# Low parts of 21 weight tiles from an adding transfer instead of a VectorE subtraction

## The chip, the core and the metric

The kernel runs on one core of a Trainium2 chip. The metric is the device time of one execution in microseconds, as the median of several runs. Engines are named as the profile names them: PE is TensorE, DVE is VectorE, ACT is ScalarE, POOL is GpSimd and SP is SyncE.

## What is computed

A decoder of two layers on 512 positions of width 1024, in f32. A layer has a first gated feed-forward part, a token mixer (layer 0: latent attention beside gated linear attention, layer 1: stick-breaking attention), a second feed-forward part, and a gate that adds the layer's embedding. Cut to the parts that the change touches:

```python
def rms_norm(x, w):
    return x * lax.rsqrt(jnp.mean(x * x, axis=-1, keepdims=True) + EPS) * w

def swiglu_ffn(h, w_gu, w_down):
    a, b = jnp.split(h @ w_gu, 2, axis=-1)
    return (jax.nn.silu(a) * b) @ w_down

# each layer i
x += 0.5 * swiglu_ffn(rms_norm(x, ffn1_norm), ffn1_w_gu, ffn1_w_down)
x += W_out [ MLA(h) || GLA(h) ]           # layer 0, h = rms_norm(x)
x += W_out StickBreaking(h)               # layer 1
x += 0.5 * swiglu_ffn(rms_norm(x, ffn2_norm), ffn2_w_gu, ffn2_w_down)
x += sigmoid(rms_norm(x) W_g) * (p[i] W_p)
```

## The kernel before

The activations are kept transposed: eight tiles x0 to x7 of 128 features by 512 positions. A product in f32 is made of three products in the matmul format fp32r. Each operand is split into a high part (rounded to fp32r) and a low part (the operand minus its high part), and `mm3` issues high by high (L393), high weight by low activation (L394) and low weight by high activation (L395) into one PSUM accumulator.

The weights come in tiles of 128 by up to 1024. One such tile is one block of 128 output columns with all its 1024 input rows, so it serves 24 matmuls of 512 positions. The list `plan` names the tiles in the order in which the program uses them. `weight(key)` hands out the next one and keeps two rings going ahead of it: `w_load` issues a load from SP into a raw tile wr (8 buffers, or 5 while plain tiles are loaded), and `w_split` makes the two parts, up to four tiles ahead (`WS`), in tiles wh and wl. For a plain tile `w_split` calls `w_cut`: ACT casts the high part (L260) and DVE subtracts (L261). Three tiles of the mixers' outputs and the last layer's gate are held in slabs instead (kh and kl, L313 and L314), and the groups "sg" of the feed-forward parts are combined on DVE before they are split (L289).

Three kinds of plain tile matter here:

- **"gu"**: five column blocks of gate and up projection of layer 0's first feed-forward part, ten tiles. `start` splits the first two in pieces of 256 columns (`FIRST` is 2). `gates` uses the other eight, A and B in turn. When `norm.row()` has made R, the inverse norm in all partitions (ACT's copy at L507), DVE multiplies A and B by it (L790, L793) before the nonlinearity.
- **"pg"**: the eight tiles of the gate of the embedding in layer 0 (`ple`), used as accumulators G. DVE's instructions in this stage are kept in program order, and the profile puts all of them at L123. Behind the gate the next norm's steps run: nu, nw and their parts (nuh by ACT at L562), and the sum of squares sqa, which TensorE reduces at L587.
- **"oo"**: the output projection of the odd mixer (layer 1). Tiles 0 to 2 are held in slabs, tiles 3 to 7 are plain. They are taken while the attention heads still run: a head makes scores z, soft values u (ACT L1508 to L1510, DVE L1512), their parts soh and sol, sums la of u over column blocks by POOL (L1521, L1522), whose parts are lah (ACT L399) and lal (DVE L401), and the next head's sqk with parts sqkh and sqkl. TensorE reads lal at L1537 and sqkl at L395.

The order on each engine is set by the scheduler that lays out the program, from what each instruction depends on and which ring buffers come free; an engine works through its list in that order and waits on semaphores. POOL has little to do in the kernel: the la sums, some casts of constants and a few loads that it issues (L376).

Of the kernel before, what the change touches and what calls it, by code (L numbers as in the profile page):

```python
# [13 lines left out]
AF = mybir.ActivationFunctionType  # L14
ALU = mybir.AluOpType
# [93 lines left out]
def tile_kernel(ctx: ExitStack, tc: tile.TileContext, a: dict, out: bass.AP):  # L109
    nc = tc.nc  # L110
    act, dve, pe, pool = nc.scalar, nc.vector, nc.tensor, nc.gpsimd
# [27 lines left out]
    def sl(p, dt=F32):  # L139
        return slab.tile([P, S], dt, tag="s", name=nm(p))  # L140
# [4 lines left out]
    def bank(p="ps"):  # L145
        return ps.tile([P, S], F32, tag="b", name=nm(p))

    def f32(t):
        return t.bitcast(F32)


    plan = []
# [70 lines left out]
    raw, ready = {}, {}  # L223
    at = [0, 0, 0]
    FIRST = 2
# [3 lines left out]
    loads, needs, done = [], [], []  # L229
    base, grouped = {}, set()  # L230
    for key in plan:
# [7 lines left out]
        if g not in base:  # L239
# [3 lines left out]
            n = 2 * groups_of(w_, l_)[g_][1]  # L243
            src = a[f"sg{w_}{l_}{g_}"]
# [14 lines left out]
    def w_cut(t, n, hi, lo, cs, pin=lambda ins: ins):  # L259
        pin(act.copy(hi[:, cs], t[:, cs]))  # L260
        pin(dve.tensor_tensor(lo[:, cs], t[:, cs], f32(hi)[:, cs], op=ALU.subtract))  # L261

    def w_tiles():
        hi = wp.tile([P, WCOLS], F32R, tag="wh", name=nm("wh"), bufs=WS)
        lo = wp.tile([P, WCOLS], F32R, tag="wl", name=nm("wl"), bufs=WS)
        return hi, lo

    def kept(i):

        k = plan[i]  # L270
        return k[0] == "pgl" or (k[0] in ("eo", "oo") and k[1] < OPEN)

    def wc(w, o):
        return w[o // S][:, o % S : o % S + P] if isinstance(w, list) else w[:, o : o + P]

    def w_pin(key):


        if key[3] == 0 and key[4] == "T1":
            return tc.keep_in_program_order  # L280
        return lambda ins: ins

    def w_term(key):

        _, _, _, _, term, u = key
        b0 = base[key[:4]]
        (b11, n), (b21, _), (b12, _), (b22, _) = [raw.get(b0 + 2 * b + u, (None, 0)) for b in range(4)]
        pin = w_pin(key)
        sub = lambda o, x, y: pin(dve.tensor_tensor(o[:, :n], x[:, :n], y[:, :n], op=ALU.subtract))  # L289
        if term == "T1":  # L290
            sub(b11, b12, b11)
        elif term == "T2":
            sub(b11, b22, b11)
        elif term == "T3":
            sub(b12, b22, b12)
        elif term == "T4":
            sub(b21, b21, b11)
        return {"B11": b11, "B21": b21, "T1": b11, "T2": b11, "B22": b22, "T3": b12, "T4": b21}[term], n

    def w_split():  # L300
        i = at[1]
        if plan[i][0] == "sg":
            t, n = w_term(plan[i])
            ready[i] = w_tiles()
            w_cut(t, n, *ready[i], slice(0, n), w_pin(plan[i]))
            at[1] += 1
            return
        t, n = raw.pop(needs[i] - 1)
        if kept(i):
            parts = [[sl("kh", F32R) for _ in range(2)], [sl("kl", F32R) for _ in range(2)]]  # L310
            for c in range(2):
                src = t[:, c * S : c * S + S]
                act.copy(parts[0][c], src)  # L313
                dve.tensor_tensor(parts[1][c], src, f32(parts[0][c]), op=ALU.subtract)  # L314
            ready[i] = parts
        else:
            ready[i] = w_tiles()
            w_cut(t, n, *ready[i], slice(0, n))
        at[1] += 1

    def weight(*key):
        assert plan[at[2]] == key, (plan[at[2]], key)
        while True:
            of = done[at[1] - 1] if at[1] else 0
            if at[0] < len(loads) and at[0] - of < (WR if at[0] in grouped else WR_PLAIN):
                w_load()
            elif at[1] < len(plan) and at[1] < at[2] + WS and needs[at[1]] <= at[0]:
                w_split()
            else:
                break  # L330
        k = plan[min(at[1], len(plan) - 1)][0]
        for _ in range(BURST.get(k, 0)):
            if at[1] < at[2] + AHEAD and at[1] < len(plan) and needs[at[1]] <= at[0] and kept(at[1]):
                w_split()
        got = ready.pop(at[2])
        at[2] += 1
        return got
# [302 lines left out]
    def start(norm):  # L640

        table("silu_and_others")
        warm = bank("warm")
        for _ in range(WARM):
            pe.matmul(warm, ones_r, ones_r[:, 0:1].to_broadcast([P, S]), start=True, stop=True)
# [1011 lines left out]
def groups_of(w, l):  # L1657

    if (w, l) == (1, 0):
        return [(KC * P, 384), (KC * P + 384, 384)]  # L1660
    return [(0, 512), (512, 512), (1024, 384)]
# [10 lines left out]

EV = (0, 2, 4, 6, 1, 3, 5, 7)
OPEN = 3
WARM = 8
AHEAD = 5
BURST = {"eo": 2, "oo": 1, "pgl": 1}
# [56 lines left out]
def build(arrays):  # L1734
    import concourse.bacc as bacc

    nc = bacc.Bacc("TRN2", target_bir_lowering=False, num_devices=1, dynamic_dma_scratch_size=4096)
    a = {
        n: nc.dram_tensor(f"in_{n}", list(v.shape), mybir.dt.from_np(v.dtype), kind="ExternalInput").ap()
        for n, v in arrays.items()  # L1740
    }
    out = nc.dram_tensor("out", [S, D], F32, kind="ExternalOutput").ap()
    with tile.TileContext(nc) as tc:
        tile_kernel(tc, a, out)
    return nc
# [9 lines left out]
```

## Time and profile before

| | |
|---|---|
| median of three runs | 1315.92 us |
| the three runs | 1312.94, 1319.41, 1315.92 us |
| the profiled execution | 1318.16 us |
| its span, first to last instruction | 1316.4 us |
| busy PE, DVE, ACT, POOL | 1280.7, 910.8, 665.1, 116.9 us |
| DVE's subtractions at L261, all weights | 292 rows, 312.7 us |
| ACT's casts at L260 | 299 rows, 275.4 us |

All rows are of the one profiled execution. A row of a timeline gives the start, the duration, the engine, the line, the operation with what it writes and reads, and in brackets how long the engine had been idle and what released it. Where several like instructions follow one another the row gives their number and their whole time. A matmul's duration overlaps the next one's, so the distance of starts is the rate. Lines of kept instructions of DVE are shown as L123.

### The profile page before, as it was taken

The page shows a single profiled execution, that of the slowest core. Times are in us where ns is not written, and L with a number is a line of the kernel's source. Part 1 is how long each engine was busy: PE and PEld are TensorE (multiplying, and loading weights), DVE is VectorE, ACT ScalarE, POOL GpSimd, SP SyncE. Part 2 cuts the span into 40 slices and gives each one's busy share as a digit, 9 for nine tenths or more (in the row PEclk, how much of TensorE's full clock was granted, in tenths as well). Part 3 has the DMA queues.
Part 4 walks back from the last instruction along what each step waited for, and adds up shares of the span by engine and source line. Part 5 has one row for each costly group of instructions (what it writes and reads, how often), then busy time and mean ns, then how long its engine had stood idle before and what let it go on. Part 6 is the DMA issues. An engine that isn't in the chain of part 4 may idle for free.

```text
span 1316.4 us, 16266 instructions
## 1 busy us (share of the span) xinstructions
PE 1280.7 (97%) x6212; PEld 1092.2 (83%) x6212; DVE 910.8 (69%) x1316; ACT 665.1 (51%) x1064; POOL 116.9 (9%) x132
## 2 busy tenths in 40 slices
PE   9969999998999999999989999999999999999997
PEld 7869888886888888988868898888888887898886
DVE  6688763579775998654799875445767598885544
ACT  6455352432654565542655553334778556554442
POOL 0001000425350000000000000000111000000000
PEclk9979999999899999999989999999999999999999
DMA  7023343111300032533203343322113003224401
GB/s 290 34 88 117 109 147 106 45 64 41 121 17 17 0 128 97 160 128 111 81 1 128 97 129 111 128 97 96 65 59 102 16 16 128 93 85 142 145 1 64
DMA packets 39454, 118.66 MB, mean 90 GB/s; under 512 B 4615, under 2 KB 5768, under 8 KB 39376
## 3 DMA queue, kind: packets, MB, share of 16 engines
q1 hardware_dynamic: 38016, 114.64, 26.2%
q0 software_dynamic: 640, 1.89, 0.5%
q8 instruction: 49, 0.80, 0.2%
q10 hardware_dynamic: 720, 1.09, 0.2%
q14 instruction: 29, 0.24, 0.1%
HBM read 115.50 MB, written 2.10 MB: 89 GB/s over the span
## 4 chain that ended last, share of the span: by engine, by line
PE 87%; DVE 9%; ACT 2%; issue 1%; SPq 0%; DMA 0%; POOL 0%; POOLq 0%; DVEq 0%; ACTq 0%
PE dn L395 6%; PE dn L394 6%; PE dn L393 6%; PE al L704 5%; PE al L705 5%; PE al L706 5%; PE ga L705 3%; PE ga L704 3%; PE ga L706 3%; PE sqk L393 2%; PE sqk L395 2%; PE sqk L394 2%; PE val L1016 2%; PE val L1018 2%; PE val L1017 2%; DVE wl L261 1%
## 5 line engine op out<-in xcount | busy, mean ns | idle before, releaser
L260 ACT CAST wh<-wr 128x1024 fp32r<-128x1024 f32 (+3 forms) x299 | 275.4, 925 | 362.2 <-PE dn L394 81.5
L261 DVE TENSOR_TENSOR wl<-wr,wh 128x1024 fp32r<-128x1024 f32 (+3 forms) x292 | 312.7, 1075 | 168.1 <-ACT wh L260 167.4
L395 PE MATMUL dn<-gh,wl 128*128 128x512 f32 x352 | 137.4, 390 | 0.3 <-DVE wl L261 0.2
L393 PE MATMUL dn<-gh,wh 128*128 128x512 f32 x352 | 137.0, 392 | 0.7 <-ACT wh L260 0.7
L394 PE MATMUL dn<-gl,wh 128*128 128x512 f32 x352 | 137.2, 390 | 0.0
L289 DVE TENSOR_TENSOR wr<-wr,wr 128x1024 f32<-128x1024 f32 (+1 forms) x88 | 94.9, 1097 | 0.2
L395 PEld LDWEIGHTS dn<-gh,wl 128*128 128x128 f32 x352 | 66.1, 188 | 14.9 <-DVE wl L261 1.2
L393 PEld LDWEIGHTS dn<-gh,wh 128*128 128x128 f32 x352 | 66.0, 188 | 14.5 <-ACT wh L260 1.1
L394 PEld LDWEIGHTS dn<-gl,wh 128*128 128x128 f32 x352 | 66.1, 188 | 13.8 <-DVE gl L401 0.6
L602 POOL TENSOR_TENSOR rc<-v,half 128x4 f32<-128x4 f32 x8 | 11.8, 1480 | 683.5 <-DVE v L600 683.5
L704 PE MATMUL al<-wh,nvh 128*128 128x512 f32 (+1 forms) x176 | 64.6, 367 | 4.7 <-ACT nvh L534 4.7
L705 PE MATMUL al<-wl,nvh 128*128 128x512 f32 (+1 forms) x176 | 64.5, 366 | 0.0
L706 PE MATMUL al<-wh,nvl 128*128 128x512 f32 (+1 forms) x176 | 64.3, 367 | 0.0
L637 DVE SCALAR_TENSOR_TENSOR x<-dn,x 128x512 f32<-128x512 f32 x32 | 22.1, 691 | 40.9 <-PE dn L395 40.9
L393 PE MATMUL sqk<-xnh,wh 128*128 128x512 f32 x128 | 50.2, 393 | 0.0
L395 PE MATMUL sqk<-xnh,wl 128*128 128x512 f32 x128 | 50.0, 390 | 0.0
L394 PE MATMUL sqk<-xnl,wh 128*128 128x512 f32 x128 | 49.9, 390 | 0.0
L704 PE MATMUL ga<-wh,nuh 128*128 128x512 f32 (+1 forms) x88 | 34.6, 406 | 6.3 <-ACT wh L260 6.3
L704 PEld LDWEIGHTS al<-wh,nvh 128*128 128x128 f32 x176 | 33.2, 189 | 8.9 <-ACT nvh L534 5.1
L481 ACT ACTIVATE sq<-x 128x512 f32<-128x512 f32 x64 | 39.2, 622 | 0.0
L1016 PE MATMUL val<-wh,xnh 128*128 128x512 f32 x96 | 37.5, 391 | 0.0
L1018 PE MATMUL val<-wh,xnl 128*128 128x512 f32 x96 | 37.4, 389 | 0.0
(462 smaller groups left out, 3293.6 us busy)
## 6 DMA issues: line engine op xcount, KB each, us to landing
wr<-in_sg SPq DMA_DIRECT2D x48, 512.0 KB, 4.0
wr<-in_sg SPq DMA_DIRECT2D x40, 384.0 KB, 3.3
wr<-in_dn SPq DMA_DIRECT2D x32, 384.0 KB, 3.1
wr<-in_dn SPq DMA_DIRECT2D x32, 320.0 KB, 3.5
wr<-in_od_qk SPq DMA_DIRECT2D x16, 512.0 KB, 3.2
wr<-in_ev_in SPq DMA_DIRECT2D x12, 512.0 KB, 3.5
wr<-in_gu SPq DMA_DIRECT2D x8, 512.0 KB, 7.2
wr<-in_ev_out SPq DMA_DIRECT2D x8, 512.0 KB, 3.2
```

The costliest lines, as they stand in the source:

```text
L260: pin(act.copy(hi[:, cs], t[:, cs]))
L261: pin(dve.tensor_tensor(lo[:, cs], t[:, cs], f32(hi)[:, cs], op=ALU.subtract))
L289: sub = lambda o, x, y: pin(dve.tensor_tensor(o[:, :n], x[:, :n], y[:, :n], op=ALU.subtract))
L393: pe.matmul(acc, wh, xh, start=start, stop=False, **k)
L394: pe.matmul(acc, wh, xl, start=False, stop=False, **k)
L395: pe.matmul(acc, wl, xh, start=False, stop=stop, **k)
L481: ins = act.activation(sq, x[m], AF.Square)
L704: pe.matmul(o, h[:, cs], wh[:, ws], start=begin, stop=False, skip_group_check=True)
L705: pe.matmul(o, h[:, cs], wl[:, ws], start=False, stop=False, skip_group_check=True)
L706: pe.matmul(o, lw[:, cs], wh[:, ws], start=False, stop=end, skip_group_check=True)
L1016: pe.matmul(accs[b], xn[k][0][:, bs], wh[:, ws], start=k == 0, stop=False)
L1018: pe.matmul(accs[b], xn[k][1][:, bs], wh[:, ws], start=False, stop=k == KD - 1)
```

## The change

The new function `w_cut_dma` makes the two parts of a tile without DVE. ACT casts the high part as before, ACT writes its negative into the low part's tile, and POOL issues a transfer that reads the weight once more from memory and adds it onto that tile. `w_split` calls it for every plain tile of "pg", "oo" and "gu" except the two of `start`: eight of "gu", eight of "pg" and five of "oo". What is kept in slabs, and all other weights, are split as before.

```diff
+    def w_cut_dma(t, src, n, hi, lo):
+        act.copy(hi[:, :n], t[:, :n])
+        act.activation(lo[:, :n], f32(hi)[:, :n], AF.Copy, scale=-1.0)
+        pool.dma_start(lo[:, :n], src, accum_op=ALU.add)
...
             ready[i] = parts
+        elif plan[i][0] in BY_DMA and needs[i] > FIRST:
+            ready[i] = w_tiles()
+            w_cut_dma(t, loads[needs[i] - 1][0], n, *ready[i])
         else:
             ready[i] = w_tiles()
             w_cut(t, n, *ready[i], slice(0, n))
...
+BY_DMA = ("pg", "oo", "gu")
```

Over the program DVE has 21 rows fewer, ACT 21 more and POOL 21 more, and SP's list is the same. In the new program L260 stands for the casts of `w_cut`, L279 and L280 for the cast and the negation of `w_cut_dma`, L281 for its transfer; later lines are ten higher. The scheduler also moves rows on the other engines. Three places follow; the numbers behind a name count its buffers and differ between the two programs.

The first is PE in `gates`, at the first tile that `start` did not split: A_61 with wh_31 and wl_32, then B_65 and A_69 with the next tiles. Before:

```order
L393 MATMUL A_61_296<-xnh_10_127,wh_31_236 128x512
L394 MATMUL A_61_296<-xnl_11_129,wh_31_236 128x512
L395 MATMUL A_61_296<-xnh_10_127,wl_32_237 128x512
L393 MATMUL A_61_296<-xnh_12_141,wh_31_236 128x512
L394 MATMUL A_61_296<-xnl_13_143,wh_31_236 128x512
L395 MATMUL A_61_296<-xnh_12_141,wl_32_237 128x512
L393 MATMUL A_61_296<-xnh_14_155,wh_31_236 128x512
L394 MATMUL A_61_296<-xnl_15_157,wh_31_236 128x512
```

Now:

```order
L403 MATMUL A_61_300<-xnh_10_127,wh_31_236 128x512
L404 MATMUL A_61_300<-xnl_11_129,wh_31_236 128x512
L403 MATMUL B_65_332<-xnh_10_127,wh_34_243 128x512
L404 MATMUL B_65_332<-xnl_11_129,wh_34_243 128x512
L403 MATMUL A_69_364<-xnh_10_127,wh_37_250 128x512
L404 MATMUL A_69_364<-xnl_11_129,wh_37_250 128x512
L405 MATMUL A_61_300<-xnh_10_127,wl_32_237 128x512
L403 MATMUL A_61_300<-xnh_12_141,wh_31_236 128x512
L404 MATMUL A_61_300<-xnl_13_143,wh_31_236 128x512
L405 MATMUL A_61_300<-xnh_12_141,wl_32_237 128x512
```

The first products of the next two accumulators are moved ahead of the first one that reads wl_32.

The second is POOL in the odd mixer, the sixth and the seventh of the eight heads (la_1884 and la_1887 are the sixth's, la_1931 and la_1934 the seventh's). Before:

```order
L1521 COPY la_1884_8634<-u_1876_8608 128x128
L1522 TENSOR_TENSOR la_1884_8634<-u_1876_8608,u_1875_8607 128x128
L1521 COPY la_1887_8641<-u_1875_8607 128x128
L1522 TENSOR_TENSOR la_1887_8641<-u_1875_8607,la_1884_8634 128x256
L1521 COPY la_1931_8823<-u_1923_8797 128x128
L1522 TENSOR_TENSOR la_1931_8823<-u_1923_8797,u_1922_8796 128x128
L1521 COPY la_1934_8830<-u_1922_8796 128x128
L1522 TENSOR_TENSOR la_1934_8830<-u_1922_8796,la_1931_8823 128x256
```

Now:

```order
L281 DMA wl_1945_8885<-in_od_out 128x1024
L1531 COPY la_1884_8650<-u_1876_8624 128x128
L1532 TENSOR_TENSOR la_1884_8650<-u_1876_8624,u_1875_8623 128x128
L281 DMA wl_1949_8908<-in_od_out 128x1024
L1531 COPY la_1887_8657<-u_1875_8623 128x128
L1532 TENSOR_TENSOR la_1887_8657<-u_1875_8623,la_1884_8650 128x256
L281 DMA wl_1965_8980<-in_od_out 128x1024
L281 DMA wl_1987_9072<-in_od_out 128x1024
L1531 COPY la_1931_8839<-u_1923_8813 128x128
L1532 TENSOR_TENSOR la_1931_8839<-u_1923_8813,u_1922_8812 128x128
L1531 COPY la_1934_8846<-u_1922_8812 128x128
L1532 TENSOR_TENSOR la_1934_8846<-u_1922_8812,la_1931_8839 128x256
```

Four transfers now stand between the la operations: of tile 3 ahead of the first pair, of tile 4 ahead of the second, of tiles 5 and 6 ahead of the four of the seventh head.

The third is ACT at the end of the embedding's gate, where wh_1282 and wh_1299 are weights of the next feed-forward part and nuh belongs to its norm. Before:

```order
L260 CAST wh_1282_5799<-wr_1187_5389 128x1024
L546 ACTIVATE noh_1263_5735<-x3_75,gains_70 128x512
L813 ACTIVATE gt_1271_5773<-gt_1271_5773 128x512
L260 CAST wh_1299_5867<-wr_1195_5436 128x1024
L562 CAST nuh_1272_5780<-nu_1265_5738 128x512
L563 CAST nwh_1252_5679<-nw_1251_5678 128x256
L481 ACTIVATE sq_1273_5783<-x3_75 128x512
L546 ACTIVATE noh_1274_5787<-x5_77,gains_70 128x512
```

Now:

```order
L556 ACTIVATE noh_1263_5751<-x3_75,gains_70 128x512
L260 CAST wh_1282_5815<-wr_1187_5401 128x1024
L823 ACTIVATE gt_1271_5789<-gt_1271_5789 128x512
L572 CAST nuh_1272_5796<-nu_1265_5754 128x512
L573 CAST nwh_1252_5695<-nw_1251_5694 128x256
L491 ACTIVATE sq_1273_5799<-x3_75 128x512
L260 CAST wh_1299_5883<-wr_1195_5448 128x1024
L556 ACTIVATE noh_1274_5803<-x5_77,gains_70 128x512
```

The cast of wh_1299 is moved behind nuh_1272 and the two instructions after it; noh_1263 comes ahead of wh_1282.

## Rows read from the trace of the kernel before

**Rows 1.** The page: busy time by engine, and the chain that ended last.
```profile
PE 1280.7 (97%) x6212; PEld 1092.2 (83%) x6212; DVE 910.8 (69%) x1316; ACT 665.1 (51%) x1064; POOL 116.9 (9%) x132
...
PE 87%; DVE 9%; ACT 2%; issue 1%; SPq 0%; DMA 0%; POOL 0%; POOLq 0%; DVEq 0%; ACTq 0%
```

**Rows 2.** Windows; columns: us, PE, PEld, DVE, ACT, POOL busy, clock, DMA share, GB/s.
```profile
0.00:43.00 43.00, 41.19 (x169) 32.33 (x170) 24.81 (x40) 22.64 (x34) 2.99 (x8) 1.00 0.66 238
...
992.00:1003.70 11.70, 11.70 (x59) 9.92 (x58) 8.69 (x14) 11.43 (x23) 2.29 (x4) 1.00 0.41 134
1013.30:1020.90 7.60, 7.60 (x36) 6.28 (x35) 5.11 (x9) 7.60 (x16) 2.30 (x4) 1.00 0.23 73
```

**Rows 3.** Timeline of DVE; columns: start us, us, line, operation, [idle before <-releaser].
```profile
43.26 0.68 DVE L790 TENSOR_TENSOR a<-A,R 128x512 f32<-128x512 f32 x1
...
654.57 1.23 DVE L123 TENSOR_TENSOR wl<-wr,wh 128x1024 fp32r<-128x1024 f32 x1 [0.57 <-ACT wh L260]
...
667.33 0.69 DVE L123 TENSOR_TENSOR nul<-nu,nuh 128x512 fp32r<-128x512 f32 x1 [0.93 <-ACT nuh L562]
...
1004.27 0.89 DVE L401 TENSOR_TENSOR lal<-la,lah 128x256 fp32r<-128x256 f32 x2
...
1008.43 0.69 DVE L401 TENSOR_TENSOR sqkl<-sqk,sqkh 128x512 fp32r<-128x512 f32 x1 [0.69 <-ACT sqkh L399]
...
1062.76 0.69 DVE L635 TENSOR_TENSOR x<-x,oo 128x512 f32<-128x512 f32 x1 [0.65 <-PE oo L395]
```

**Rows 4.** Timeline of ACT: casts of the third plain gate tile and the first pg.
```profile
15.20 1.05 ACT L260 CAST wh<-wr 128x1024 fp32r<-128x1024 f32 x1 [0.42 <-DMA wr<-in_gu]
...
602.42 1.06 ACT L260 CAST wh<-wr 128x1024 fp32r<-128x1024 f32 x1 [2.35 <-PE dn L394]
```

**Rows 5.** Timeline of POOL: a transfer issued from it.
```profile
81.46 0.61 POOL L376 DMA_DIRECT2D craw<-in_consts  x1 [44.51 <-DVE nwl L569]
```

**Rows 6.** Transfers: KB each, median us to landing.
```profile
wr<-in_gu SPq DMA_DIRECT2D x8, 512.0 KB, 7.2
wr<-in_pg SPq DMA_DIRECT2D x8, 512.0 KB, 3.2
...
craw<-in_consts POOLq DMA_DIRECT2D x3, 256.0 KB, 3.1
```

**Rows 7.** Timeline of PE: third tile's first products, and pg's first low part.
```profile
18.35 0.39 PE L393 MATMUL A<-xnh,wh 128*128 128x512 f32 x1
18.58 0.39 PE L394 MATMUL A<-xnl,wh 128*128 128x512 f32 x1
...
613.06 0.39 PE L395 MATMUL G<-xnh,wl 128*128 128x512 f32 x1
```

**Rows 8.** Timeline of PE behind the embedding's gate.
```profile
685.42 1.75 PE L587 MATMUL pss<-ones,sqa 128*128 128x2 f32 x8 [1.98 <-DVE sqa L123]
```

**Rows 9.** Windows behind three stops of PE.
```profile
299.00:306.00 7.00, 6.71 (x37) 5.74 (x38) 6.78 (x17) 1.08 (x2) 0.00 (x0) 1.00 0.01 2
685.00:692.50 7.50, 7.08 (x21) 5.56 (x22) 6.85 (x9) 5.53 (x8) 1.92 (x1) 0.54 0.00 1
1090.00:1096.00 6.00, 5.46 (x20) 4.13 (x21) 6.00 (x8) 4.72 (x6) 1.93 (x1) 0.72 0.00 0
```

**Rows 10.** Timeline of ACT behind the last plain gate tile.
```profile
41.99 0.58 ACT L507 COPY R<-wide 128x512 f32<-128x512 f32 x1
```

**Rows 11.** Timeline of POOL in the odd mixer, sixth head.
```profile
1000.58 0.76 POOL L1521 COPY la<-u 128x128 f32<-128x128 f32 x1
1001.30 0.91 POOL L1522 TENSOR_TENSOR la<-u,la 128x256 f32<-128x256 f32 x1
```

**Rows 12.** Timeline of ACT in the odd mixer, sixth head.
```profile
1002.91 0.82 ACT L399 CAST lah<-la 128x256 fp32r<-128x256 f32 x2
```

**Rows 13.** Timeline of PE in the odd mixer, sixth head.
```profile
1008.06 0.34 PE L1537 MATMUL z<-lal,cr 128*128 128x384 f32 x1
...
1011.35 0.34 PE L395 MATMUL z<-sqkh,sqkl 128*128 128x384 f32 x1
```

## The prediction

> **What bounds the kernel now.** The page first: TensorE is busy for 97% of the span, VectorE for 69%, and the chain that ended last is 87% TensorE and 9% VectorE [rows 1]. So freed VectorE time is worth something only where TensorE waits for VectorE. The windows by stage come next, since the 21 tiles lie in three places: in the first 43 us TensorE is busy for 41.19 us while VectorE needs 24.81, and the DMA engines are busy for 0.66; in two stretches of the odd mixer TensorE never stops, and ScalarE is busy for 11.43 of 11.7 us and for all of 7.6 us [rows 2]. There the change adds work to a full engine and takes it from one that has room. The timelines then give lengths and waits one by one.
>
> **What is removed.** 21 subtractions of 1.23 us (each as the one at 654.57 [rows 3]) leave VectorE, some 26 us. The eight of the plain gates gain nothing: TensorE is the full engine there. The eight of the embedding's gate gain nothing: VectorE waits 0.57 us for ScalarE's high part at 654.57, and what it was ahead by is lost again. The five of the odd mixer's output stand beside a TensorE without a gap, and at 1062.76, behind the last of them but one product, VectorE waits 0.65 us for TensorE [rows 3]. So the removal gains 0, and its cover is TensorE's own work; without that cover the two waits of 0.57 and 0.65 us are what stands between VectorE and a gain.
>
> **What is added.** First 21 negations on ScalarE, taken as the cast of the same tile, 1.05 us [rows 4], of which I count 0.95 when they follow one another. Then 21 transfers of 512 KB that POOL issues behind the negation. No view of before shows an adding transfer. Its issue I take from POOL's plain one, 0.61 us [rows 5], with 0.5 and 2 as bounds. For the time to landing the nearest rows are 3.2 us for a plain 512 KB of the embedding's gate, 3.1 for 256 KB from POOL, and 7.2 for the plain gates' 512 KB while SP loads without pause [rows 6]. The low bound is 3.2, the high one two loaded transfers, 14.4. I take 6, nearest to the loaded row, because the first ones run in the window where the DMA engines are 0.66 busy.
>
> The Trainium skill ("Collectives: The Full Stack", section on the bandwidth ceiling) says that a reducing transfer is slower not for the addition but for its two source reads, which halve the rate. By it the 3.2 us would become up to 6.4, an estimate from that page, and the sum below +8.0 instead of the +3.2 that a landing like the plain row gives; no run so far shows which.
>
> **The plain gates.** Tile 2 is cast at 15.20 [rows 4]; TensorE begins with it at 18.35, a product every 0.23 us [rows 7], 24 to a tile. In the new order it runs six products ahead (two each of tiles 2, 3 and 4), work for 6 x 0.227 = 1.36 us, to 19.71; the seventh reads tile 2's low part. Cast and negation end at 17.2, and 6 us later it is 23.2: delay 23.2 - 19.7 = **+3.5**. The low bound is not 3.2 of landing (20.4, or +0.7) but ScalarE: tile 4's cast is now fifth in its row and ends at 15.20 + 4 x 0.95 + 1.05 = 20.05, its two products at 20.5, or +0.8. The high bound is 17.2 + 14.4 = 31.6, or +11.9. The other seven tiles are cut up to three tiles ahead of use, some 5.4 us (24 x 0.227) each, and cost nothing.
>
> **The clock behind that stop.** TensorE would stop for some 3 us. Behind its stop for mq at 299 the granted clock over 7 us is 1.00; behind the stop of 1.98 us at 685.42 [rows 8] it is 0.54 over 7.5 us; behind that at 1090 it is 0.72 over 6 us [rows 9]. At 1.00 it is the level of 2.4 GHz, and half of it that of 1.2. The losses are 0, 7.5 x 0.46 = 3.4 and 6 x 0.28 = 1.7 us; I take the middle one, **+1.7**, and 0 and 3.4 as bounds.
>
> **The end of the plain gates.** ScalarE copies R at 41.99 directly behind the last cast [rows 10]; now a negation stands between, and R is there at 43.5 instead of 42.6. VectorE used it at 43.26 [rows 3], behind the subtraction that is gone: **+0.3** (0 to 0.35).
>
> **The embedding.** VectorE waits 0.93 us for nuh at 667.33 [rows 3], which stood on ScalarE behind a cast, and then works on to the sqa for which TensorE stops 1.98 us at 685.42 [rows 8]. In the new order nuh stands ahead of that cast: **-0.9** (0; or -2.5, with part of the clock's drop behind it). The gate's first tile is cast at 602.42 [rows 4] and its low part read at 613.06 [rows 7]: behind negation and issue some 8 us are left for the landing, and 6 fit: 0.
>
> **The odd mixer.** POOL's la operations, four per head, now queue behind adding transfers that wait for ScalarE's negations. The sixth head today: the later la pair takes from 1000.58 to 1002.21 [rows 11], lah is cast from 1002.91 [rows 12], lal is ready at 1005.16 and the second sqkl at 1009.12 [rows 3]; TensorE reads them at 1008.06 and 1011.35 [rows 13]. That is 2.9 and 2.2 us of slack. ScalarE has hardly a gap there, so the negation for the output's tile 3 moves all behind it by 0.95. That for tile 4 stands where lah stood and ends at 1002.91 + 0.95 + 1.05 = 1004.9; then come the issue, 0.61, the la pair, 1.63, lah's second half, 0.5, and lal's, 0.55: 1008.2, 3.0 us late. The sqkl behind it is as late: 3.0 - 2.2 = +0.8, or +0.9 with the small gaps. In the seventh head the transfers of tiles 5 and 6 stand ahead of all four la operations instead of two. I take +2.1 there, a choice between the same +0.9 and the whole 3.0. Together **+3.0** (1.8 to 3.9; with 2 us for an issue up to 6). TensorE's waits there are 1 to 2 us at a time, for which I count no clock.
>
> **The sum.** 3.5 + 1.7 + 0.3 - 0.9 + 3.0 = +7.6 us. The profiled execution took 1318.16 us, 2.2 above the median of 1315.92, with a span of 1316.4. It would become 1325.8, the median **1323.5**. By itself the likeliest case reaches from 1320 to 1328.
>
> **The rivals.**
>
> A, not slower: an adding transfer lands like a plain one, in 3.2 us. TensorE then stops for under 1 us at the start and its clock stays: 0.8 + 0 + 0.3 - 0.9 + 3.0 = +3.2, or 1319.1. It decides where the landing is under 4 us. For it: POOL's own queue shows 3.1. Against it: the loaded row, 7.2. Chance 0.27.
>
> B: the landing takes two loaded transfers, 14.4 us: 11.9 + 3.4 + 0.3 - 0.9 + 3.0 = +17.7, or 1333.6. For it: the loaded row; against it: most rows are near 3.2. Chance 0.11.
>
> C: POOL needs 2 us for an issue. The start loses 1.4 more and the odd mixer 3: +12.0, or 1327.9. Against it: the plain issue's 0.61. Chance 0.11.
>
> D: the first adding transfer waits in full behind the loads that SP has in flight, 7.2 us, and takes 1 us more for itself. Delay 17.2 + 8.2 - 19.7 = 5.7, clock 3.4: 5.7 + 3.4 + 0.3 - 0.9 + 3.0 = +11.5, or 1327.4. For it: the DMA engines are 0.66 busy. Against it: it is another queue. Chance 0.08. The Trainium skill ("DMA: Bandwidth & Descriptors", section "Queues, rings and completion order") says that an engine takes from its queues in turn, packet by packet; by that it would share with SP's loads and come in ahead of some of them, as in the likeliest case.
>
> E, faster by over 0.5%, which is 6.6 us and about what a measurement can tell from no change: freed VectorE time would have to end TensorE's waits in places that I do not see. Even with A's start, nothing lost in the odd mixer, and the stop at 685.42 gone with its clock, it is 0.8 + 0.3 - 2.0 - 3.4 = -4.3, or 1311.6. Chance 0.04.
>
> That the change does not do what it says is excluded by the order: VectorE has 21 subtractions fewer, ScalarE 21 operations more and POOL 21 transfers.
>
> **Chances.** Likeliest 0.39, A 0.27, B 0.11, C 0.11, D 0.08, E 0.04. The bound for slower is 1322.5; of the likeliest case 0.25 lie above it and 0.14 below. Slower is 0.25 + 0.11 + 0.11 + 0.08 = 0.55, faster 0.04, the same 0.41. The range takes in A with its spread of 4 us below and C and D above, and most of B: 1315 to 1335.
>
> **What would show it.** Busy time of VectorE down by some 25 us and of ScalarE up by 20. In the list of transfers, wl from three inputs on POOL's queue, about 6 us to landing. At 20 to 23 us a stop of TensorE for wl, with the clock below 1.00 behind it. Near 667 no wait for nuh. Between 1000 and 1030 stops of TensorE for lal or sqkl, about 1 us in the sixth head and 2 in the seventh. The forecast is wrong if TensorE doesn't stop near 20 us, or stops for wl in the embedding's gate, or if POOL's issues take over 1 us.

## The result and the profile after

The changed kernel takes 1325.58 us (median of six runs, 1323.25 to 1328.88), the kernel before 1315.16 us (six runs, 1312.94 to 1319.53). The ratio is 1.0077 with a 95% interval of 1.006 to 1.0093: slower by 10 us, between 8 and 12. The forecast was 1323.5, +7.6 us. The interval lies wholly above 0.5%, the side that had the chance of 0.55. The profiled execution took 1328.88 us, with a span of 1327.1, and is the slowest of the six; the lengths below are read inside it, the totals from the medians.

The page first: busy times, two of the transfer queues (packets, MB, share of 16 engines' span), and the chain that ended last.

```profile
PE 1282.4 (97%) x6212; PEld 1091.4 (82%) x6212; DVE 887.4 (67%) x1295; ACT 684.5 (52%) x1085; POOL 132.6 (10%) x153
...
q1 hardware_dynamic: 38016, 114.64, 26.1%
q0 software_dynamic: 3664, 12.90, 5.3%
...
PE 83%; DVE 10%; ACT 3%; DMA 1%; issue 1%; POOL 0%; SPq 0%; POOLq 0%; DVEq 0%; ACTq 0%
```

Against [rows 1], VectorE has 23 us less and ScalarE 19 us more; TensorE, with the same matmuls, is busy 2 us longer; and the chain has 83% TensorE where it had 87%, with 3% ScalarE where it had 2% and 1% DMA where it had none. VectorE's part of the chain did not shrink with the work that left it, 10% where it was 9%. Queue q0, which is POOL's, moved 1.89 MB for 0.5% in the kernel before. So 11.0 MB more of it cost 4.8% of the engines, 0.44% for a MB, where SP's q1 costs 26.1 / 114.64 = 0.23%: an added megabyte takes 1.9 times the engine time of a loaded one.

Then TensorE's list of waits (us in total, times, longest).

```profile
PE A L405 <- DMA wl<-in_gu: 5.5, 1, 5.5
...
PE pss L597 <- DVE sqa L123: 3.6, 1, 3.6
...
PE A L403 <- ACT wh L279: 1.3, 1, 1.3
...
PE z L403 <- ACT ea L1553: 0.8, 1, 0.8
...
PE z L403 <- ACT sqkh L409: 0.3, 1, 0.3
```

Of these the waits for wl, for wh at L279, for ea and for sqkh are new; that for sqa was 1.98 us [rows 8]. The largest is at the third tile of the plain gates, as the timeline of PE shows:

```profile
17.57 0.39 PE L403 MATMUL A<-xnh,wh 128*128 128x512 f32 x1
...
20.33 0.50 PE L403 MATMUL A<-xnh,wh 128*128 128x512 f32 x1 [1.29 <-ACT wh L279]
20.67 0.39 PE L404 MATMUL A<-xnl,wh 128*128 128x512 f32 x1
26.58 0.80 PE L405 MATMUL A<-xnh,wl 128*128 128x512 f32 x1 [5.51 <-DMA wl<-in_gu]
27.17 0.63 PE L403 MATMUL A<-xnh,wh 128*128 128x512 f32 x1
...
30.57 0.39 PE L405 MATMUL A<-xnh,wl 128*128 128x512 f32 x1
```

and POOL's timeline, with the issue of the transfer that it waits for:

```profile
17.63 0.90 POOL L281 DMA_DIRECT2D wl<-in_gu  x1 [3.63 <-ACT wl L280]
```

The tile's first product stands at 17.57, where it stood at 18.35 in the profile before [rows 7]. Six products are issued ahead, the last two only behind a wait of 1.29 us for the third cast, and at 20.9 TensorE stops until 26.58. The transfer was issued at 17.63, so it was some 8.9 us under way. Behind the stop nine products fill the time from 26.58 to the tenth's start at 30.57: 3.99 us instead of 9 x 0.227 = 2.04.

The windows of that stretch say why (columns as in [rows 2]); first the kernel before, then the one after.

```profile
18.00:22.00 4.00, 4.00 (x20) 3.30 (x19) 3.74 (x4) 3.76 (x6) 0.00 (x0) 1.00 1.01 413
22.00:26.00 4.00, 4.00 (x19) 3.34 (x18) 2.74 (x5) 2.67 (x5) 0.00 (x0) 1.00 1.04 419
```

```profile
18.00:22.00 4.00, 1.66 (x5) 0.59 (x4) 0.00 (x0) 3.97 (x5) 1.39 (x2) 1.00 1.06 399
22.00:26.00 4.00, 0.00 (x0) 0.00 (x0) 1.59 (x3) 3.73 (x7) 1.71 (x2) 0.71 1.02 262
26.00:30.00 4.00, 3.42 (x8) 2.75 (x9) 1.18 (x2) 0.00 (x0) 0.00 (x0) 0.50 1.06 263
```

In both the DMA engines are full. Before, a full set of engines moved 413 to 419 GB/s. From 22 us on, with adding transfers beside SP's loads, the same full engines move some 260. The clock falls from 1.00 to 0.71 and to 0.50, the level of 1.2 GHz.

### The profile page after: what moved, and what is told of

Same layout as the page of the kernel before. It is cut to its first block, busy times and chain, and to the rows that moved or that the text cites. A ratio compares the mean times of both kernels' runs of the same rounds, so it can differ in the third digit from the quotient of the medians.

```text
span 1327.1 us, 16324 instructions
## 1 busy us (share of the span) xinstructions
PE 1282.4 (97%) x6212; PEld 1091.4 (82%) x6212; DVE 887.4 (67%) x1295; ACT 684.5 (52%) x1085; POOL 132.6 (10%) x153
## 3 DMA queue, kind: packets, MB, share of 16 engines
q1 hardware_dynamic: 38016, 114.64, 26.1%
## 4 chain that ended last, share of the span: by engine, by line
PE 83%; DVE 10%; ACT 3%; DMA 1%; issue 1%; POOL 0%; SPq 0%; POOLq 0%; DVEq 0%; ACTq 0%
PE dn L405 6%; PE dn L404 6%; PE dn L403 6%; PE al L714 5%; PE al L716 5%; PE al L715 5%; PE ga L715 3%; PE ga L714 3%; PE ga L716 3%; PE sqk L403 2%; PE sqk L405 2%; PE sqk L404 2%; PE val L1026 2%; PE val L1027 2%; PE val L1028 2%; DVE wl L261 1%
## 5 line engine op out<-in xcount | busy, mean ns | idle before, releaser
L260 ACT CAST wh<-wr 128x1024 fp32r<-128x1024 f32 (+3 forms) x278 | 253.1, 915 | 328.2 <-PE dn L404 78.0
L261 DVE TENSOR_TENSOR wl<-wr,wh 128x1024 fp32r<-128x1024 f32 (+3 forms) x275 | 292.9, 1069 | 158.9 <-ACT wh L260 157.9
L403 PEld LDWEIGHTS dn<-gh,wh 128*128 128x128 f32 x352 | 66.1, 188 | 14.4 <-ACT wh L260 1.1
L1027 PE MATMUL val<-wl,xnh 128*128 128x512 f32 x96 | 37.4, 390 | 0.0
```

The costliest lines, as they stand in the source:

```text
L403: pe.matmul(acc, wh, xh, start=start, stop=False, **k)
L1027: pe.matmul(accs[b], xn[k][0][:, bs], wl[:, ws], start=False, stop=False)
```

## The experiments

Each run was timed beside the kernel before on the same chip; a ratio r stands for 1315 x (r - 1) us. The medians of the kernel before in these sets were 1313.98 (first four), 1314.94 (next four) and 1315.21 (last two). Where the text says how far TensorE falls back in a stretch, the n-th product of a run's profile is set against the n-th of the profile before, with times of the profile before.

**One place at a time.** Three kernels make only one of the three kinds by transfer, and a fourth leaves out the first three gu tiles:

```diff
-BY_DMA = ("pg", "oo", "gu")
+BY_DMA = ("gu",)          # or ("pg",), or ("oo",)
```

```diff
-        elif plan[i][0] in BY_DMA and needs[i] > FIRST:
+        elif plan[i][0] in BY_DMA and needs[i] > FIRST + 3:
```

The plain gates alone:

> Only the eight tiles of the plain gates by adding transfer. Theory (the first tile's landing): TensorE stops some 5 us for wl near 21 us and 1 to 2 us for the casts ahead of it, the clock drops behind it, and the whole is +9.5 us (1324.7). Rival (every adding transfer costs alike, 10.4 us over 21 by its extra reading): 8 x 0.5 = +4.0 us (1319.2).

Measured: 1323.89 us, ratio 1.0076 (1.0064 to 1.0088), +10.0 us. The embedding's gate alone:

> Only the eight tiles of the embedding's gate by adding transfer. Theory: nothing waits for these transfers, and nuh ahead of the cast gives 1.0 us, with part of a clock drop near 680 some 2.5: -1 to -2.5 us (1312.7 to 1314.2). Rival (every adding transfer costs alike): +4.0 us (1319.2).

Measured: 1313.91 us, ratio 0.9993 (0.9979 to 1.0007), -0.9 us, not told from none. The odd mixer's output alone:

> Only the five tiles of the odd mixer's output by adding transfer. Theory (ScalarE's negations and POOL's queue delay la and lal): TensorE waits in the sixth and seventh head, +2.7 us (1317.9), all between 1000 and 1035 us. Rival (every adding transfer costs alike): 5 x 0.5 = +2.5 us, but spread, without waits of TensorE in these heads; third view (freed VectorE time is worth something here): 0 or less.

Measured: 1316.98 us, ratio 1.0020 (1.0009 to 1.0030), +2.6 us. In its profile TensorE falls back by 2.8 us between 1005 and 1035, and by nothing else from 700 to 1085: not spread, as the first rival had it, but in the heads. The last five gu tiles alone:

> Only the last five of the plain gates' eight tiles by adding transfer, the first three by VectorE as before. Theory: only the first tiles are late, so TensorE doesn't stop near 20 us and the time is that of before, up to +0.5 us for R behind the last negation (1315.2 to 1315.7). Rival (every adding transfer costs alike): 5 x 0.5 = +2.5 us (1317.7).

Measured: 1314.95 us, ratio 1.0005 (0.9994 to 1.0016), +0.7 us, not told from none.

So an equal price for each transfer is out: eight in the gates cost 10.0 us, five of these eight 0.7, and eight in the embedding nothing that can be told from none. The three kinds add to 10.0 - 0.9 + 2.6 = 11.7 us, and the whole change measured 10.1 (8 to 12). Almost all of the gates' cost comes with the first three tiles, and the timeline of PE of the kernel with the gates alone has the same two stops as the changed one:

```profile
21.05 0.50 PE L403 MATMUL A<-xnh,wh 128*128 128x512 f32 x1 [1.29 <-ACT wh L279]
...
27.25 0.79 PE L405 MATMUL A<-xnh,wl 128*128 128x512 f32 x1 [5.46 <-DMA wl<-in_gu]
```

**What makes the first transfer slow: the addition.** The same kernel, same order on every engine, but with a plain write instead of the addition.

```diff
-        pool.dma_start(lo[:, :n], src, accum_op=ALU.add)
+        pool.dma_start(lo[:, :n], src.bitcast(F32R))
```

> As the run with the plain gates alone, but the transfer from POOL writes the weight instead of adding it (the addition is left out, so the low part is the whole weight). Same order on every engine. Theory (the addition's second reading makes the landing long): landing falls from 7.5 us median to 4 to 5, the stop for wl near 21 us from 5.5 to about 2, and the time from +9.9 to some +5 us (1319). Rival (SP's loads on the same engines make it long): landing and stop stay within 1 us of 7.5 and 5.5, time +9 to +10 us (1323 to 1324).

Measured: 1323.70 us, ratio 1.0060 (1.0040 to 1.0081), +7.9 us. Its list of transfers and its timeline of PE:

```profile
wl<-in_gu POOLq DMA_DIRECT2D x8, 512.0 KB, 5.8
```

```profile
25.05 0.80 PE L405 MATMUL A<-xnh,wl 128*128 128x512 f32 x1 [3.75 <-DMA wl<-in_gu]
```

The median landing falls from 7.5 us in the run above to 5.8, that of the first transfer from 8.9 to 7.2, and the stop from 5.46 to 3.75. Both sides expected too much of one cause: the addition is 1.7 us of the stop, and without it 3.75 us of stop and most of the loss stay. The intervals of the two times overlap (8.4 to 11.6 and 5.3 to 10.7), so this reading rests on the two profiles: in them TensorE falls back by 10.3 and by 7.7 us between 18 and 25.

The two pages also say what an added megabyte costs the engines. Queue q0 with the addition, then with the plain write:

```profile
q0 software_dynamic: 1792, 6.08, 2.3%
```

```profile
q0 software_dynamic: 1792, 6.08, 1.6%
```

Less the 1.89 MB and 0.5% that it has in the kernel before, that is 0.43% and 0.26% for a MB. So it is the addition that costs the engines more, and not POOL's queue.

**What makes it slow: the loads beside it.** SP's loads from the sixth gu tile on wait until the first adding transfer has landed:

```diff
+            if held and i < 16:
+                dve.tensor_copy(t[0:1, 0:1], f32(held[0])[0:1, 0:1])
             nc.sync.dma_start(t[:, :n], src)
...
         pool.dma_start(lo[:, :n], src, accum_op=ALU.add)
+        if not held:
+            held.append(lo)
...
-            if at[0] < len(loads) and at[0] - of < (WR if at[0] in grouped else WR_PLAIN):
+            if at[0] < len(loads) and at[0] - of < (3 if not held else WR if at[0] in grouped else WR_PLAIN):
```

> The plain gates alone by adding transfer, with SP's loads from the sixth gu tile on held back until the first adding transfer has landed (a one-element write that reads its result). Theory (the landing is long because SP's loads fill the DMA engines): the first transfer lands in 5 to 6.5 us after its issue, as in the embedding's gate, instead of 8.9; the stop for wl falls from 5.5 to about 2.5 to 3 us, and the time from +9.9 to +6 to +7.5 us (1320 to 1321.5), if no later tile comes late. Rival (the addition alone makes it long): landing over 8 us, stop over 5 us, time +9 us or more.

Measured: 1321.15 us, ratio 1.0036 (1.0019 to 1.0053), +4.7 us. Its POOL, PE and window rows:

```profile
18.16 0.92 POOL L283 DMA_DIRECT2D wl<-in_gu  x1 [4.33 <-ACT wl L282]
```

```profile
23.70 0.79 PE L409 MATMUL A<-xnh,wl 128*128 128x512 f32 x1 [2.11 <-DMA wl<-in_gu]
```

```profile
18.00:22.00 4.00, 2.06 (x7) 0.76 (x5) 0.00 (x0) 3.84 (x4) 1.79 (x2) 0.99 0.59 88
```

With the engines at 0.59 instead of full, the transfer that is issued at 18.16 has landed by 23.7, after 5.5 us, and the stop is 2.11 us. So of the 5.5 us of stop in the kernel with the gates alone, some 3.4 come from SP's loads on the same engines.

The packets show in which way. The queues of the changed kernel from the first issue at 17.63 on, for two windows of its list of transfers, 17.6 to 21.7 and 24 to 25 us:

```profile
q1 hardware_dynamic: 459, 1.66, 102.0%
```

```profile
q0 software_dynamic: 35, 0.14, 71.5%
q1 hardware_dynamic: 35, 0.13, 35.7%
```

For 4.1 us no packet of POOL's queue q0 moves, while SP's q1 fills the engines. Then the packets of the two queues come one for one, and one of q0 takes twice the time of one of q1. In this run, the held one, with the engines idle, the first packet moves 1.6 us after the issue, and so it does behind each of the five issues of the odd mixer in the changed kernel (1.57 to 1.63). So of the 8.9 us of the first transfer some 1.6 pass in any case, 2.5 behind packets of SP, and 4.8 in moving beside them, where the held run takes 3.9. What stays is the chain of cast, negation, issue and a landing of 5.5 us, longer than the work that TensorE has ahead.

By the ratio the time came out below what the theory gave, 4.7 (2.5 to 7.0) instead of 6 to 7.5. But nine of the 23 executions of the kernel before in this last set took 1319 us or more, at a mean granted clock of 0.982 (0.983 to 0.989 in the others); likely it is the drop of the clock that the last section tells of, which the profiled execution before has at 1318.16 us and 0.983. The other fourteen have a median of 1313.7, and against that the run is at +7.4. In its profile TensorE falls back by 6.9 us between 18 and 25, within what the theory gave.

**What costs 2.6 us in the odd mixer.** Two edits. In the first, VectorE makes the la sums, so that nothing waits behind the transfers on POOL; its control is the kernel before with the same edit.

```diff
-                pool.tensor_copy(sm[:, :P], own[:, :P])
-                pool.tensor_tensor(sm[:, P:n], own[:, P:], t, op=ALU.add)
+                dve.tensor_copy(sm[:, :P], own[:, :P])
+                dve.tensor_tensor(sm[:, P:n], own[:, P:], t, op=ALU.add)
```

> Odd mixer's output by adding transfer, and the la sums made by VectorE, so that nothing on POOL stands behind the transfers. Theory (ScalarE's negation and POOL's queue share the cost): the stops for sqkh and sqkl go, the one for ea, behind the negation of tile 5, stays: +1.0 to +1.5 us (1315.0 to 1315.5). Rival 1 (POOL's queue alone): 0 (1314.0). Rival 2 (ScalarE alone): +2.6 us as with POOL (1316.6).

> The kernel before with the la sums made by VectorE, the control of the run above: all theories expect no change, 1313.5 to 1314.5 us, since VectorE has room in the heads and slack behind la is over 2 us.

Measured: 1321.12 us with the transfers (ratio 1.0044, 1.0030 to 1.0057) and 1321.07 for the control (1.0049, 1.0033 to 1.0064). The control was to show nothing and is 6.4 us slower than the kernel before, so the pair doesn't separate the views. VectorE has become what TensorE waits for in these heads, through ScalarE's cast of la, as the control's list of waits of ScalarE from 930 to 1050 us and its timeline of PE show:

```profile
ACT lah L399 <- DVE la L1522: 15.6, 14, 1.7
```

```profile
1041.88 0.38 PE L1537 MATMUL z<-lah,cr 128*128 128x256 f32 x1 [0.66 <-ACT lah L399]
```

ScalarE's list of the kernel before has no wait for la in this stretch. Between 900 and 1050 TensorE falls back by 4.4 us in the control, and by 6.7 with the transfers; with one profile of each and the same time for both, what the transfers cost there stays open.

In the second, VectorE makes the negation, and the la sums stay on POOL behind the transfers:

```diff
-        act.activation(lo[:, :n], f32(hi)[:, :n], AF.Copy, scale=-1.0)
+        dve.tensor_scalar(lo[:, :n], f32(hi)[:, :n], -1.0, None, op0=ALU.mult)
```

> Odd mixer's output by adding transfer, the negation made by VectorE instead of ScalarE; POOL's la sums stand behind the transfers as before. Theory (ScalarE's negation and POOL's queue share the cost): the stop for ea goes, those of the sixth head shrink to under 0.5 us since POOL now waits only for a cast and VectorE: 0 to +1.0 us (1314 to 1315). Rival 1 (POOL's queue alone): +2 to +2.6 us (1316 to 1316.6). Rival 2 (ScalarE alone): 0.

Measured: 1314.89 us, ratio 0.9999 (0.9983 to 1.0014): nothing, within -2.2 and +1.8 us, and in its timeline TensorE has no wait between 1005 and 1030 us; it falls back by 0.2 us between 1005 and 1035, where it was 2.8 with ScalarE's negation. The transfers still stand ahead of la operations on POOL, so its queue by itself costs nothing that can be measured; it cost where it passed on a delay of ScalarE. The operation that takes the negation's place, in the groups of instructions of 985 to 1040 us, is short:

```profile
L280 DVE TENSOR_SCALAR wl<-wh 128x1024 fp32r<-128x1024 f32 x4 | 2.8, 694 | 1.3 <-ACT wh L279 1.2
```

**The change without its two costs.** The first three gu tiles by VectorE, the odd mixer's negations by VectorE, 18 tiles by transfer:

```diff
-        act.activation(lo[:, :n], f32(hi)[:, :n], AF.Copy, scale=-1.0)
+        if by == "oo":
+            dve.tensor_scalar(lo[:, :n], f32(hi)[:, :n], -1.0, None, op0=ALU.mult)
+        else:
+            act.activation(lo[:, :n], f32(hi)[:, :n], AF.Copy, scale=-1.0)
...
-        elif plan[i][0] in BY_DMA and needs[i] > FIRST:
+        elif plan[i][0] in BY_DMA and needs[i] > FIRST + 3:
```

> The whole change without its two costs: the first three gu tiles by VectorE, the negations of the odd mixer's output by VectorE, everything else by adding transfer (18 tiles). Theory (VectorE is not what TensorE waits for, so its freed 16 us are worth nothing): no stop near 20 us and none in the heads, time as before, 0 to -1 us (1313 to 1315). Rival (the two costs hid a gain of the removal): -3 us or more (below 1312).

Measured: 1314.30 us beside 1315.21, ratio 0.9984 (0.9969 to 0.9998), -2.1 us by the ratio and -0.9 by the medians. Its busy times:

```profile
PE 1274.8 (97%) x6212; PEld 1086.8 (83%) x6212; DVE 895.0 (68%) x1303; ACT 677.0 (52%) x1077; POOL 130.7 (10%) x150
```

VectorE has 16 us less than before [rows 1], and by the ratio the kernel gains 0.3 to 4 us of 1315. That gain is not shown to come from the freed time: it is measured against the set in which nine of the 23 executions of the kernel before took 1319 us or more, none of the twelve of this kernel did, and against the median of the other fourteen, 1313.7, it is 0.6 us slower. TensorE has no stop near 20 us nor in the heads, as the theory had it. The freed time is worth little, as the forecast had it, though not shown to be exactly nothing.

## Why the prediction was right, step by step

The direction, the range and the three places were right. The size was short by 2.5 us (7.6 where 10.1 was measured). The term that was mis-sized is the landing of the first transfer; it was short by more than that, and the places measured one by one add to 11.7.

- **The removal gains nothing.** Right. The eight tiles of the embedding, which lose a subtraction each, measured -0.9 us with an interval across zero, and 16 us off VectorE with both costs mended gave at most 4, and nothing against the fourteen executions.
- **The plain gates, +3.5 us.** The mechanism was right, TensorE stops at the seventh product; the size was the term that failed. The landing was taken as 6 us "because the first ones run in the window where the DMA engines are 0.66 busy". That 0.66 is a mean over 43 us. In the 8 us that mattered the engines were full. The first transfer took 8.9 us, and 26.58 - (17.57 + 1.36) = 7.65 us were lost instead of 3.5. Of the 4.15 that this is more, 2.95 are the landing, 0.43 the issue, which came at 17.63 and not with the negation's end at 17.2, and 0.78 come from TensorE, which reached the tile that much earlier in this execution than in the profile before. The rows for a better value were there: a loaded row of 7.2 that I should have taken as the plain case and lengthened for the addition, not shortened: the first plain write from POOL took 7.2, the first adding transfer 8.9. The bound from ScalarE held: the third pair of products began at 20.33, behind a cast that was forecast to end at 20.05.
- **The addition.** Row and rule were to be weighed: a landing as the plain row, 3.2, or up to 6.4. Without SP's loads beside it the first adding transfer lands in 5.5 us in the held run; medians are 6.5 us in the embedding and 5.2 in the odd mixer (the list of transfers below). An added megabyte takes 1.9 times the engine time of one that SP loads, and 1.6 times that of one that POOL writes; the 260 GB/s where 413 to 419 stood are those of a mix with SP's loads. What the Trainium skill says in "Collectives: The Full Stack", section on the bandwidth ceiling, that two source reads halve the rate, agrees with that 1.9.

```profile
wl<-in_gu POOLq DMA_DIRECT2D x8, 512.0 KB, 7.7
...
wl<-in_pg POOLq DMA_DIRECT2D x8, 512.0 KB, 6.5
...
wl<-in_od_out POOLq DMA_DIRECT2D x5, 512.0 KB, 5.2
```

- **The clock, +1.7 us.** Near: 3.99 us for nine products that take 2.04, so 1.95 lost. The other profiles lose 2.8 (the gates alone), 1.6 (the plain write) and 2.5 (the held run) behind the same stop, all within the bounds of 0 and 3.4; the middle one of three losses was a choice.
- **R behind the negation, +0.3 us.** VectorE's multiplication by R comes late as worked out, at 52.55, 9.29 us behind its place at 43.26 [rows 3], while TensorE's products stand 8.86 behind. But they stand 8.8 to 8.9 behind from 25 to 60 us: TensorE didn't wait for it, and for the time the term was nothing.

```profile
52.55 0.69 DVE L800 TENSOR_TENSOR a<-A,R 128x512 f32<-128x512 f32 x1 [5.12 <-ACT R L517]
```

- **The embedding, -0.9 us.** The wait for nuh at nul is gone, as the timelines of DVE and of PE show:

```profile
676.83 0.69 DVE L123 TENSOR_TENSOR nul<-nu,nuh 128x512 fp32r<-128x512 f32 x1
```

```profile
694.91 1.05 PE L597 MATMUL pss<-ones,sqa 128*128 128x2 f32 x8 [3.61 <-DVE sqa L123]
```

  The product for sqa stands 9.5 us behind its place at 685.42 [rows 8], while the products of 655 us stand 10.5 us behind theirs in the two timelines: 1.0 us gained. TensorE gains it ahead of that, at the first products ga of the next part, whose stop for wh falls from 1.28 to 0.3 us. It stops for sqa longer than before, 3.61 us, because it arrives earlier. By the whole time this is not told from none (-2.8 to +0.9 us).
- **The odd mixer, +3.0 us.** Right in sum: +2.6 (1.2 to 3.9). The division was off. The sixth head was forecast at +0.9 through lah and sqkh, and that is about what it lost: TensorE stands 8.1 us behind at 1005 and 9.0 ahead of the stop for ea. ScalarE and POOL did what was worked out: the negation at 1011.80, the issue behind it, the second lah only at 1015.06.

```profile
1011.80 1.06 ACT L280 ACTIVATE wl<-wh 128x1024 fp32r<-128x1024 f32 x1
1012.76 0.39 ACT L409 CAST lah<-la 128x256 fp32r<-128x256 f32 x1
1015.06 0.51 ACT L409 CAST lah<-la 128x384 fp32r<-128x384 f32 x1 [1.91 <-POOL la L1532]
...
1020.83 1.06 ACT L280 ACTIVATE wl<-wh 128x1024 fp32r<-128x1024 f32 x1
...
1022.77 0.38 ACT L1553 ACTIVATE ea<-z 128x256 f32<-128x256 f32 x1
```

```profile
1013.15 0.88 POOL L281 DMA_DIRECT2D wl<-in_od_out  x1 [3.62 <-ACT lah L409]
1013.74 0.60 POOL L1531 COPY la<-u 128x128 f32<-128x128 f32 x1
1013.99 1.03 POOL L1532 TENSOR_TENSOR la<-u,la 128x256 f32<-128x256 f32 x1
```

  The other part, +2.1, I put down to POOL in the seventh head. Most of it is here instead; TensorE stands 10.1 behind after this stop, and 10.8 from 1035 on:

```profile
1023.20 0.50 PE L403 MATMUL z<-sqkh,sqkh 128*128 128x512 f32 x1 [0.81 <-ACT ea L1553]
```

  A product waits for a buffer of z that ScalarE's ea has to read first, and ea stood behind the negation of the next tile, at 1020.83. The run with VectorE's negations, which has no stop in the heads, shows ScalarE as the root, with the queue on POOL handing it on; that the transfers' place on POOL would cost by itself was the part of the step that fell.
- **The rivals.** A (a landing like a plain one, under 4 us) falls with medians of 5.2 us and more. C (2 us for an issue) falls with issues of 0.9 us; a plain issue from POOL takes 0.53 in the run without the addition. B (14.4 us) falls for the first transfer; the fourth did take 14.4, and TensorE did not wait for it. D (waiting in full behind SP's loads) is near in its landing, 8.2 against 8.9, and half right in its way: the first packet waits 4.1 us, 1.6 of them without SP's doing, and not 7.2, and then the transfer shares the engines with SP's loads packet by packet. The likeliest case had only the sharing; the waiting was the part of the landing that it left out. E (faster) falls with the result.

## What to carry to other kernels

A step taken off an engine that nothing waits for gained nothing that could be told here, and what replaced it was paid where it met a full engine: here ScalarE in the heads and the DMA engines in the first 40 us. Before work is moved onto transfers, the DMA engines' share is to be read in the few microseconds of the first use, not in the mean of a stage, a transfer that adds is to be counted as two in the engines' time, and one from another queue can stand for microseconds until loads that are under way let its first packet through. The first tile of a ring has little work ahead of it to hide a longer path; the later ones have.

## What had not been expected

- The la sums on VectorE instead of POOL cost 6.4 us by the ratio (medians 1321.07 and 1314.94), though VectorE was busy for only 7 us more in all (918.2 and 910.8). Where a chain of three engines ends in a matmul, the room on an engine is not the slack of its chain.
- VectorE's negation of a 128x1024 tile takes 0.69 us, the subtraction of the two tiles 1.23 us [rows 3]; negated there, a tile costs VectorE over half of what it saves.
- Executions differ by some 5 us in places that no edit touches. After TensorE's stops for mq near 320 us the clock fell to 0.56 between 326 and 336 us in the profile before and was 1.00 there in the profile of the five late gu tiles, which had 0.83 in the 10 us ahead of it. That is why the single profiles' spans here don't order the kernels. A median moves too with the share of such executions, as in the last set.
